# A decoder block's first stage: column sums on TensorE and VectorE against row sums from transposed weights on VectorE

## The chip, the cores and the metric

The kernel runs on one core of a Trainium2 chip. The metric is the device time of one execution in microseconds (us), given as the median of several runs; a profile of one execution supplies all durations of single instructions. The core's engines are TensorE (PE, matmuls; PEld is its weight load), VectorE (DVE), ScalarE (ACT), GpSimd (POOL) and SyncE (SP), which issues the DMA transfers. Each works through a queue of its own in the order of the program and waits on semaphores of the others.

## The reference

One decoder block on 1024 tokens of width 1024, batch 1, all in fp32. Only the first lines concern the change; attention and MLP follow.

```python
cond = jax.nn.silu(c)
mod = (cond @ w_ada[l] + b_ada[l]).astype(x.dtype)          # 1024 -> 6 * 1024
sh_a, sc_a, gt_a, sh_m, sc_m, gt_m = [m[:, None, :] for m in jnp.split(mod, N_MOD, axis=-1)]
h = rms_norm(x, g_attn_pre[l]) * (1 + sc_a) + sh_a
proj = h @ w_in[l]                                          # 1024 -> 2304
...
y = mixed @ w_out[l]                                        # after two attentions, with RoPE on q and k
x = x + gt_a * rms_norm(y, g_attn_post[l])
h = rms_norm(x, g_mlp_pre[l]) * (1 + sc_m) + sh_m
y = jnp.square(jax.nn.relu(h @ w_up[l])) @ w_down[l]
x = x + gt_m * rms_norm(y, g_mlp_post[l])
```

## The kernel before

A scheduler in Python writes the whole program. Each piece of work is an `op` with an engine (or a choice of two), an estimated duration, the ops it depends on and the buffers it takes and gives back; a planner with its own clock then lays down the order of every engine's queue. So a change in one piece can move instructions that it does not touch. Rings of buffers are counted by `Res` objects: `r_stg` and `r_wa` for loaded 512 KB pieces, `r_w` for split weights, `r_t`, `r_x`, `r_pj`, `r_o`, `r_s` for the eight PSUM banks (tags t, x, pj, o, s). Loads made with `in_turn` are issued strictly in the order of the code.

Products that need fp32 accuracy are made of three matmuls. Each operand is split into a high part (rounded by a cast on ScalarE) and a low part (the rest, by a subtraction); then high x high, high x low and low x high add up in one bank. Lines 773, 774 and 776 are these three.

The first stage, up to the first scores at about 93 us:

- **x**: eight blocks of 128 rows. Each is squared and summed on ScalarE (L571), `rs_t` is formed on VectorE (L409), its power -1/2 on GpSimd (L412), the block is scaled (L575 on ScalarE or L576 on VectorE), transposed by eight matmuls (L583, `pxt`), and copied into `xnT` (L587), the transposed x.
- **Angles** of RoPE: 27 dependent steps on 64 elements a partition, on GpSimd (L539 to L546), some last ones on VectorE (L552 to L555), then sine tables on ScalarE (L559 to L561).
- **Modulation**: the first 2048 columns of w_ada (shift and scale of attention) come in four groups of columns, each in four pieces of 512 KB. Some pieces go through TensorE against `cond` with one column moving (L609, table `BY_PE`); the others are multiplied by a column of cond and added up on VectorE (L624, L626 into `acc_a`), and the sum over partitions is a matmul against ones (L635). L640 to L642 make the scale `g_a` and the shift `s_a` of two chunks of 128 columns.
- **Modulated block**, for each chunk k of 128 columns: the high part of `xnT * g_a + s_a` on ScalarE (L652, `hw`), the full value on VectorE (L655), the low part on GpSimd or VectorE (L658).
- **Weights**: w_in is cut into six units of 384 columns (two heads of one kind with their keys and values, or four with one key head). A unit's eight chunks are loaded (L477 and on, `w_st`), split into `w_hl` by a cast on ScalarE (L494) and a subtraction (L499, for unit 0 on GpSimd).
- **Projection of unit 0**: seven of the eight row blocks (`FIRST`) accumulate side by side, each in a bank of its own (`acc_at`), for chunks 0 to 5 chunk by chunk; chunks 6 and 7 follow row block by row block (`AHEAD` = 6), so that the first block is done early. The eighth row block is a normal tile. Each finished block goes to ScalarE and VectorE, through rotation, transposes of q and k (`pq` L726, `pk` L738, in bank x) and on to the scores (`s_ps`, L999).

Units 1 to 5 and the two attentions are then interleaved, until about 450 us; the output projection and the MLP follow.

## Time and profile before

| what | us |
|---|---|
| median of 3 runs (1200.5 to 1203.06) | 1202.58 |
| span of the profiled execution, first to last instruction | 1198.4 |
| first cast of a modulated chunk (L652) starts | 30.7 |
| last one starts | 70.4 |
| first scores (L999) | 92.77 |
| mean granted TensorE clock over the span | 0.978 |

The page cuts the span into 40 slices of 30 us. Each digit is the busy share of a slice in tenths.

```profile
PE   6889999999998998999899999999999999999996
DVE  5867768666779897666888965479763797646998
POOL 5536455565655333111100000000000000000002
PEclk8689999999999999999999999999999999999999
DMA  9512332323331413555297127951268511585103
```

The change concerns the first three digits. In the second slice, 30 to 60 us, TensorE's granted clock is 0.6.

### The profile page before, as it was taken

Reading aid. Unit: us, or ns where it says so; the run is one execution under the profiler, and the core shown is the slowest. Engines: PE = TensorE matmul, PEld = TensorE weight load, DVE = VectorE, ACT = ScalarE, POOL = GpSimd, SP = SyncE. Lnnn points to the kernel's source line nnn. Section 1 sums busy time; section 2 is a strip of 40 time slices with the busy share of each in tenths; the row PEclk is TensorE's granted clock in tenths of the full one; section 3 lists DMA queues with packets and bytes.
Section 4 is the critical chain, followed back from the end, with each engine's and each line's share of the span. In section 5 each row is a group of like instructions: output and inputs, shape, how many; then the busy total and the mean of one; then the engine's idle time right before and its main releaser. Section 6 shows DMA issues by size and latency. Waiting matters only on the chain.

```text
span 1198.4 us, 17398 instructions
## 1 busy us (share of the span) xinstructions
PE 1148.6 (96%) x6060; PEld 1001.4 (84%) x6060; DVE 885.4 (74%) x1773; ACT 660.2 (55%) x1390; POOL 266.1 (22%) x322
## 2 busy tenths in 40 slices
PE   6889999999998998999899999999999999999996
PEld 5888999989998896888688888888888888888885
DVE  5867768666779897666888965479763797646998
ACT  6328666566566787567657533474324643246542
POOL 5536455565655333111100000000000000000002
PEclk8689999999999999999999999999999999999999
DMA  9512332323331413555297127951268511585103
GB/s 311 167 56 64 88 99 77 85 62 91 87 87 54 121 52 80 180 186 209 105 380 261 36 71 227 339 180 55 78 224 285 193 36 53 177 286 221 36 18 141
DMA packets 96488, 166.54 MB, mean 139 GB/s; under 512 B 11408, under 2 KB 48400, under 8 KB 96400
## 3 DMA queue, kind: packets, MB, share of 16 engines
q1 hardware_dynamic: 96400, 165.42, 41.3%
q8 instruction: 48, 0.79, 0.3%
q14 instruction: 40, 0.33, 0.1%
HBM read 137.08 MB, written 28.31 MB: 138 GB/s over the span
## 4 chain that ended last, share of the span: by engine, by line
PE 74%; DVE 13%; ACT 4%; issue 4%; POOL 3%; DMA 3%; SPq 0%; DVEq 0%; POOLq 0%; ACTq 0%
PE mlp_ps L1775 16%; PE mlp_ps L1776 16%; PE mlp_ps L1774 16%; PE pj L773 3%; PE pj L776 3%; PE pj L774 3%; PE s_ps L999 3%; DVE acc_a L626 2%; PE o_ps L1133 1%; DMA wa<-in_w_ada 1%; PE pt_ps L1102 1%; PE y_ps L1350 1%; PE y_ps L1352 1%; PE y_ps L1351 1%; PE pt_ps L1105 1%
## 5 line engine op out<-in xcount | busy, mean ns | idle before, releaser
L1774 PE MATMUL mlp_ps<-hw 128*128 128x512 f32 x896 | 350.3, 391 | 0.4 <-ACT hw L1536 0.4
L1775 PE MATMUL mlp_ps<-hw 128*128 128x512 f32 x896 | 349.2, 390 | 1.1 <-DVE hw L1542 1.1
L1776 PE MATMUL mlp_ps<-hw 128*128 128x512 f32 x896 | 349.1, 390 | 0.0
L1775 PEld LDWEIGHTS mlp_ps<-hw 128*128 128x128 f32 x896 | 168.5, 188 | 36.8 <-DVE hw L1542 1.4
L1774 PEld LDWEIGHTS mlp_ps<-hw 128*128 128x128 f32 x896 | 168.6, 188 | 36.2 <-ACT hw L1536 0.8
L1776 PEld LDWEIGHTS mlp_ps<-hw 128*128 128x128 f32 x896 | 168.5, 188 | 35.0
L1545 DVE TENSOR_TENSOR hw<-w,hw 128x1024 fp32r<-128x1024 f32 x96 | 114.8, 1223 | 94.0 <-ACT hw L1538 92.5
L1538 ACT CAST hw<-w 128x1024 fp32r<-128x1024 f32 x96 | 97.6, 1048 | 129.6 <-PE mlp_ps L1776 93.0
L1874 POOL TENSOR_TENSOR st<-st,nhalf 128x1 f32<-128x1 f32 x8 | 7.8, 978 | 602.8 <-DVE st L1872 602.8
L773 PE MATMUL pj<-w_hl,hw 128*128 128x384 f32 x328 | 121.9, 372 | 4.1 <-DVE sk L719 4.1
L776 PE MATMUL pj<-w_hl,hw 128*128 128x384 f32 x328 | 111.3, 339 | 0.0
L774 PE MATMUL pj<-w_hl,hw 128*128 128x384 f32 x328 | 111.1, 339 | 0.0
L1538 ACT CAST hw<-u 128x1024 fp32r<-128x1024 f32 x48 | 48.7, 1054 | 64.5 <-PE mlp_ps L1776 64.5
L1120 DVE TENSOR_TENSOR ph<-pt_ps,ph 128x512 fp32r<-128x512 f32 (+1 forms) x110 | 69.2, 645 | 16.7 <-ACT ph L1116 16.2
L1545 DVE TENSOR_TENSOR hw<-u,hw 128x1024 fp32r<-128x1024 f32 x48 | 57.2, 1224 | 18.2 <-ACT hw L1538 18.2
L1116 ACT CAST ph<-pt_ps 128x512 fp32r<-128x512 f32 (+1 forms) x110 | 59.6, 561 | 14.8 <-PE pt_ps L1105 10.6
L773 PEld LDWEIGHTS pj<-w_hl,hw 128*128 128x128 f32 x328 | 62.2, 190 | 5.4 <-issue 2.9
L1029 POOL TENSOR_SCALAR p_sb<-p_sb,den 128x128 f32<-128x128 f32 (+3 forms) x64 | 49.2, 773 | 70.6 <-DVE den L1027 47.4
L1832 DVE TENSOR_TENSOR yacc<-yacc,mlp_ps 128x512 f32<-128x512 f32 x96 | 62.4, 688 | 3.3 <-PE mlp_ps L1776 3.3
L774 PEld LDWEIGHTS pj<-w_hl,hw 128*128 128x128 f32 x328 | 62.4, 190 | 1.2 <-issue 0.2
L776 PEld LDWEIGHTS pj<-w_hl,hw 128*128 128x128 f32 x328 | 62.0, 189 | 0.0
L1024 ACT ACTIVATE p_sb<-p_sb,mn 128x128 f32<-128x128 f32 (+3 forms) x64 | 50.0, 782 | 21.2 <-DVE mn L1017 17.7
(208 smaller groups left out, 2238.6 us busy)
## 6 DMA issues: line engine op xcount, KB each, us to landing
hw<-s_dram SPq DMA_DIRECT2D x84, 512.0 KB, 4.3
wa_st<-in_w_ada SPq DMA_DIRECT2D x32, 512.0 KB, 4.2
w<-in_w_up SPq DMA_DIRECT2D x32, 512.0 KB, 5.0
w<-in_w_down SPq DMA_DIRECT2D x32, 512.0 KB, 7.7
s_dram<-hw SPq DMA_DIRECT2D x28, 512.0 KB, 4.1
x_sb<-in_x SPq DMA_DIRECT2D x16, 512.0 KB, 6.1
wa<-in_w_ada SPq DMA_DIRECT2D x32, 256.0 KB, 5.8
w_st<-in_w_in SPq DMA_DIRECT2D x32, 192.0 KB, 4.7
```

The lines of the kernel that those rows point to most:

```text
L773: T.matmul(ps, hw[:, tb, 0, t], w[:, 0], start=(k == 0), stop=False)
L774: T.matmul(ps, hw[:, tb, 0, t], w[:, 1], start=False, stop=False)
L776: T.matmul(ps, hw[:, tb, 1, t], w[:, 0], start=False, stop=(k == KC - 1))
L1024: A.activation(rec.p[qi], rec.p[qi], AF.Exp, bias=b["mn"][:, m:m + 1], scale=-1.0, accum_out=b["den"][:])
L1116: A.copy(b["ph"][:, 0, :w], b["pt"][:, :w])
L1120: V.tensor_tensor(b["ph"][:, 1, :w], b["pt"][:, :w], b["ph"][:, 0, :w].bitcast(F32), ALU.subtract)
L1538: A.copy(out[j][0], flat(src[j]))
L1545: V.tensor_tensor(out[j][1], flat(src[j]), out[j][0].bitcast(F32), ALU.subtract)
L1774: T.matmul(ps[m][:], sh, mh, start=starts and k == 0, stop=False, **kw)
L1775: T.matmul(ps[m][:], sh, ml_, start=False, stop=False, **kw)
L1776: T.matmul(ps[m][:], sl, mh, start=False, stop=k == 3, **kw)
L1832: e = op("DVE", t_dv(512), lambda: V.tensor_tensor(y(), y(), ps[m][:], ALU.add), [e, ml.e_y[tb, n]], gives=gives, prio=1)
```

## The change

The host lays out two weights anew: w_in as contiguous tiles, one for each unit and chunk, and the first 2048 columns of w_ada transposed (`ada_t`: for each chunk, the output column is the partition and the 1024 inputs lie along it, once for the scale and once for the shift). With that the modulation of one output column is a sum along a partition: VectorE multiplies 128 x 1024 weights by `cond_b`, cond spread over all partitions, and adds up in the same instruction, starting from the bias (L606 of the changed kernel, `tensor_tensor_reduce`, twice a chunk). `cond_b` comes from eight matmuls of a diagonal matrix with ones.

All eight row blocks accumulate side by side in all eight banks. Block 0 takes the bank of tag x, which the transposes of q and k use later. The full value of the modulated block moves from VectorE to ScalarE, its low part and the low parts of unit 0's weights from GpSimd to VectorE, the angle steps from GpSimd to VectorE; the sine tables come after the last chunk. Unit 1's weights are loaded right behind unit 0's. Lines of the later stages stand about 24 lower than in the kernel before.

```diff
+    w = h["w_in"][0].reshape(KC, P, 2304)
+    parts = [[w[:, :, o + 128 * u:o + 128 * u + 128] for o in (768, 1280, 1792)] for u in range(4)]
+    parts += [[w[:, :, 256 * v:256 * v + 256], w[:, :, 512 + 64 * v:576 + 64 * v], w[:, :, 640 + 64 * v:704 + 64 * v]]
+              for v in range(2)]
+    h["w_in"] = np.ascontiguousarray(np.stack([np.concatenate(q, axis=2) for q in parts]))
+    a = h["w_ada"][0, :, 0:2 * D].reshape(P, KC, 2, KC, P)
+    h["ada_t"] = np.ascontiguousarray(a.transpose(3, 4, 2, 1, 0)).reshape(KC, P, 2 * D)
+    return {n: h[n] for n in ARGS}
...
-    FIRST = 7
+    FIRST = 8
...
+    cond_b = p0.tile([P, D], F32, name="cond_b")
+    NWA = 8
+
+    r_wa = Res(NWA)
     n_load = [0]
 
     def pri():
...
-    def load_ada(g, j):
-
-        def emit():
-            wa_t[g, j] = stage("wa") if j == 3 else place0("wa")
-            for n in range(2):
-                nc.sync.dma_start(
-                    wa_t[g, j][:, 512 * n:512 * n + 512].rearrange("p (i n) -> p i n", i=2),
-                    ada_view[:, 2 * j + n, 0:2 * D].rearrange("p (i n) -> p i n", i=2)[:, :, g * GW:g * GW + GW])
-        wa_e[g, j] = in_turn(emit, 524288, r_stg if j == 3 else r_wa)
+    def load_ada(k):
+        for i in (1, 0):
+            def emit(i=i):
+                wa_t[k, i] = place0("wa")
+                nc.sync.dma_start(wa_t[k, i][:], ada_t[k, :, i * D:i * D + D])
+            wa_e[k, i] = in_turn(emit, 524288, r_wa)
...
+    IN_STG = (0, 1, 2)
...
+            nc.sync.dma_start(t[:], w_in[u, k])
...
-            w_e[u, k] = op("POOL", t_ptt(UW), lo(G), [e], gives=[(r_wst, 1)], prio=3)
+            w_e[u, k] = op("DVE", t_dv(UW), lo(V), [e], gives=[(r_wst, 1)], prio=1)
...
+    e_posi = load(lambda: nc.sync.dma_start(posi[:], positions), 4096, prio=pri())
     load_x(0)
-    e_posi = load(lambda: nc.sync.dma_start(posi[:], positions), 4096, prio=pri())
     for tb in range(1, TB):
         load_x(tb)
-    for g in range(4):
-        for j in range(4):
-            load_ada(g, j)
-        for k in range(2):
-            load_w(0, 2 * g + k)
+    for k in range(KC):
+        load_ada(k)
+        load_w(0, k)
...
+    cond_ps, diag = [], []
+
+    def f_diag():
+        diag.append(by_k(place0("diag")))
+        for j in range(KC):
+            V.tensor_scalar(diag[0][:, j], ident, cond[:, j:j + 1], None, ALU.mult)
+    e = op("DVE", 1.3, f_diag, [e_cond], takes=[(r_wa, 1)], prio=0)
+
+    def f_cps():
+        for i in range(2):
+            cond_ps.append(pt.tile([P, 512], F32, name="cond_ps", tag="t"))
+            for j in range(4):
+                T.matmul(cond_ps[i][:, j * P:(j + 1) * P], ones[:], diag[0][:, 4 * i + j], start=True, stop=True)
+    e = pe_op("mod", 2.0, f_cps, [e, e_init], takes=[(r_t, 2)], gives=[(r_wa, 1)])
+
+    def f_cb():
+        for i in range(2):
+            A.copy(cond_b[:, 512 * i:512 * i + 512], cond_ps[i][:])
+    e_cb = op("ACT", 2 * t_ps(512), f_cb, [e], gives=[(r_t, 2)], prio=0)
...
-        e = op("POOL", 0.34, f, [e, e_c], prio=8)
+        e = op("DVE", 0.12, f, [e, e_c], prio=8)
...
-            junk = p0.tile([P, D], BF16, name="junk", tag="junk", bufs=1)
-            A.activation(junk[:], x_t[tb][:], AF.Square, accum_out=ssq[:, tb:tb + 1])
+            A.activation(xnT[:, :, tb * P:(tb + 1) * P], x_t[tb][:].rearrange("p (j n) -> p j n", n=P), AF.Square,
+                         accum_out=ssq[:, tb:tb + 1])
...
-    BY_PE = ((0, 2), (0,), (0,), (0,))
...
-            def f(j=j, first=first):
-                for n in range(2):
-                    w, cj = wa_t[g, j][:, 512 * n:512 * n + 512], cond[:, 2 * j + n:2 * j + n + 1]
-                    if first and not n:
-                        b["acc"] = p0.tile([P, 512], F32, name="acc_a", tag="acc_a", bufs=2)
-                        V.tensor_scalar(b["acc"][:], w, cj, None, ALU.mult)
-                    else:
...
+    e_hh, e_hl, e_full = {}, {}, [None]
+
+    def mod_chunk(k):
+
+        def gemv(i, dst, first):
+            def f():
+                w = wa_t[k, i]
+                V.tensor_tensor_reduce(w[:], w[:], cond_b[:], 1.0, first, ALU.mult, ALU.add, dst)
+            return f
+        c1 = g_a[:, k:k + 1]
+        e1 = op("DVE", t_dv(D) + AP_DV, gemv(1, c1, bb[:, k, 1:2]), [wa_e[k, 1], e_cb, e_cols],
+                gives=[(r_wa, 1)], prio=2)
+        e1 = op("DVE", 0.07, lambda: V.tensor_tensor(c1, c1, cols[:, 8 + k:9 + k], ALU.mult), [e1], prio=1)
+        e2 = op("DVE", t_dv(D) + AP_DV, gemv(0, s_a[:, k:k + 1], bb[:, k, 0:1]), [wa_e[k, 0], e_cb, e_cols],
+                gives=[(r_wa, 1)], prio=2)
...
-            V.tensor_scalar(h, h, g_a[:, k:k + 1], s_a[:, k:k + 1], ALU.mult, ALU.add)
-
-        def lo(eng):
-            return lambda: eng.tensor_tensor(hw[:, :, 1, ks], hb, hw[:, :, 0, ks].bitcast(F32), ALU.subtract)
-        e_hh[k] = op("ACT", t_sb(S) + 2 * AP_COST, hi, [eg] + e_xn, prio=0)
-        e = op("DVE", t_d2(S) + 2 * AP_DV, full, [e_hh[k]], prio=0)
-        e_hl[k] = op(("DVE", "POOL"), (t_dv(S), t_ptt(S)), (lo(V), lo(G)), [e], prio=0)
+            A.activation(h, h, AF.Identity, bias=s_a[:, k:k + 1], scale=g_a[:, k:k + 1])
+
+        def lo():
+            V.tensor_tensor(hw[:, :, 1, ks], hb, hw[:, :, 0, ks].bitcast(F32), ALU.subtract)
+        e_hh[k] = op("ACT", t_sb(S) + 2 * AP_COST, hi, [e1, e2] + e_xn, prio=0)
+        e = e_full[0] = op("ACT", t_sb(S) + 2 * AP_COST, full, [e_hh[k]], prio=0)
+        e_hl[k] = op("DVE", t_dv(S), lo, [e], prio=0)
...
-    for g in range(4):
-        mod_group(g)
+    for k in range(KC):
+        mod_chunk(k)
+
+    def f_sin():
+        A.activation(sinw[:, :, 1], ang[:], AF.Sin)
+        A.activation(cosw[:], kq[:], AF.Sin)
+        A.activation(ang[:], kq[:], AF.Exp)
+    e = op("ACT", 3.0, f_sin, [e_ang, e_full[0]], prio=8)
+    e_rope = op("DVE", 0.15, lambda: V.tensor_scalar(sinw[:, :, 0], sinw[:, :, 1], -1.0, None, ALU.mult), [e],
+                prio=8)
...
-    acc_at = [(pj, "pj", r_pj)] * 2 + [(po, "o", r_o)] + [(psp, "s", r_s)] * 2 + [(pt, "t", r_t)] * 2
+    acc_at = [(px, "x", r_x)] + [(pj, "pj", r_pj)] * 2 + [(psp, "s", r_s)] * 2 + [(po, "o", r_o)] + [(pt, "t", r_t)] * 2
...
-                      after=tick if part else None)
+                      gives=[(r_w, 1)] if part and tb == TB - 1 else [], after=tick if part else None)
...
-                load_w(u + 1, k, prio=-10 + k / 10)
+                load_w(u + 1, k, prio=-10 + k / 10 if u else None)
                 split_w(u + 1, k)
+
+    next_unit_w(0)
...
-            if tb == TB - 4 or u == 0:
+            if tb == TB - 4:
```

VectorE's order in the middle of the first stage, before: `acc_a` is the running sum over pieces of w_ada, `xnT` the transposed x, `bb` the bias; the rows end one group of two chunks and begin the next.

```order
L640 TENSOR_TENSOR g_a<-pm,bb 128x2
L641 TENSOR_TENSOR g_a<-g_a,head 128x2
L642 TENSOR_TENSOR s_a<-pm,bb 128x2
L624 TENSOR_SCALAR acc_a<-wa,cond 128x512
L626 SCALAR_TENSOR_TENSOR acc_a<-wa,cond,acc_a 128x512
L655 TENSOR_SCALAR xnT<-xnT,g_a,s_a 128x1024
L626 SCALAR_TENSOR_TENSOR acc_a<-wa,cond,acc_a 128x512 x2
```

The same place after the change; each `ISA` row of 128x1024 is one sum, the one of 128x1 the reading of its result.

```order
L606 ISA wa,g_a<-wa,cond_b,bb 128x1024
L606 ISA g_a 128x1
L495 TENSOR_TENSOR w_hl<-w_st,w_hl 128x384
L611 TENSOR_TENSOR g_a<-g_a,head 128x1
L606 ISA wa,s_a<-wa,cond_b,bb 128x1024
L606 ISA s_a 128x1
L624 TENSOR_TENSOR hw<-xnT,hw 128x8x128
```

The pieces of 512 elements for two chunks became sums of 1024 for one; the low parts L624 and L495 came in from GpSimd, and the full value L655 went out to ScalarE.

TensorE's order between the last three blocks' transposes and the first projection matmuls, before (`pm` are results of the modulation, `pxt` the transposes, numbers tell buffers apart):

```order
L583 MATMUL pxt_357<-head_65,x_sb_186 128x128 x4
L583 MATMUL pxt_366<-head_65,x_sb_186 128x128 x4
L609 MATMUL pm_381<-cond_69,wa_301 128x1 x8
L583 MATMUL pxt_406<-head_65,x_sb_188 128x128 x4
L583 MATMUL pxt_414<-head_65,x_sb_188 128x128 x4
L635 MATMUL pm_425<-ones_67,acc_a_353 128x1 x4
L583 MATMUL pxt_433<-head_65,x_sb_194 128x128 x4
L583 MATMUL pxt_445<-head_65,x_sb_194 128x128 x4
L609 MATMUL pm_451<-cond_69,wa_363 128x1 x8
L773 MATMUL acc_483<-w_hl_431,hw_126 128x384
L774 MATMUL acc_483<-w_hl_431,hw_126 128x384
```

And after:

```order
L591 MATMUL pxt_363<-head_65,x_sb_199 128x128 x4
L591 MATMUL pxt_376<-head_65,x_sb_199 128x128 x4
L591 MATMUL pxt_383<-head_65,x_sb_201 128x128 x4
L591 MATMUL pxt_395<-head_65,x_sb_201 128x128 x4
L747 MATMUL acc_414<-w_hl_381,hw_126 128x384
L748 MATMUL acc_414<-w_hl_381,hw_126 128x384
L747 MATMUL acc_422<-w_hl_381,hw_126 128x384
L748 MATMUL acc_422<-w_hl_381,hw_126 128x384
```

The modulation's matmuls are gone from between the transposes, and the projection follows the last transpose; ahead of all transposes stand eight matmuls for `cond_ps`.

GpSimd's order where the angle steps end, before:

```order
L545 TENSOR_SCALAR km<-kq 128x64
L412 TENSOR_TENSOR rstd<-rs_t,nhalf 128x1
L546 TENSOR_TENSOR ang<-ang,km 128x64
L499 TENSOR_TENSOR w_hl<-w_st,w_hl 128x384 x2
L658 TENSOR_TENSOR hw<-xnT,hw 128x8x128 x2
```

And all of it after, up to the first work on the later columns of w_ada (L860):

```order
L420 ISA
L420 TENSOR_TENSOR rstd<-rs_t,nhalf 128x1 x8
L495 TENSOR_TENSOR w_hl<-w_st,w_hl 128x384 x7
L860 TENSOR_SCALAR ada_acc<-wa_st,cond 128x512
L864 TENSOR_SCALAR wa_st<-wa_st,cond 128x512
```

The powers follow one another without angle steps between them, and the low parts of the block have left; the seven L495 belong to unit 1.

More of the change, by code (lines that the diff above doesn't have):

```diff
@@ L304, in hybrid_block @@
 def hybrid_block(ctx: ExitStack, tc: tile.TileContext, x, positions, w_ada, b_ada, g_attn_post, w_in, w_out,
-                 g_mlp_post, w_up, w_down, consts, out):
+                 g_mlp_post, w_up, w_down, ada_t, consts, out):
     nc = tc.nc
@@ L309, in hybrid_block @@
     x, out = x[0], out[0]
-    w_ada, w_in, w_out, w_up, w_down = w_ada[0], w_in[0], w_out[0], w_up[0], w_down[0]
+    w_ada, w_out, w_up, w_down = w_ada[0], w_out[0], w_up[0], w_down[0]
     sc = Sched()
@@ L556, in hybrid_block @@
     e = op("DVE", 0.8, f_ang, [e], prio=8)
-    def f_sin():
-        A.activation(sinw[:, :, 1], ang[:], AF.Sin)
-        A.activation(cosw[:], kq[:], AF.Sin)
-        A.activation(ang[:], kq[:], AF.Exp)
-    e = op("ACT", 3.0, f_sin, [e], prio=8)
-    e_rope = op("DVE", 0.15, lambda: V.tensor_scalar(sinw[:, :, 0], sinw[:, :, 1], -1.0, None, ALU.mult), [e],
-                prio=8)
+    e_ang = e
     e_xn = []
@@ L812, in proj_tile @@
                 gives.append((r_wo, 1))
-            d = dense(0.49, emit, [w_e[u, k]] + ([e_hh[k], e_hl[k]] if u == 0 else []), takes=[(r_pj, 1)] if k == 0 else [], gives=gives, after=tick)
+            d = dense(0.49, emit, [w_e[u, k]], takes=[(r_pj, 1)] if k == 0 else [], gives=gives, after=tick)
         evac(u, tb, lambda: b[0], d, r_pj)
-    todo_dense = [(u, tb) for u in range(6) for tb in range(FIRST if u == 0 else 0, TB)]
+    todo_dense = [(u, tb) for u in range(1, 6) for tb in range(TB)]
     def next_unit_w(u):
```

71 lines of the change are left out of this document (8 added, 63 removed).

## The prediction

> **What bounds the kernel now.** I read the page's engine row first, then a table of busy time by stretches of the span, then the first stage by its timeline. An engine's field in the table is busy us (instructions); the last three fields are TensorE's granted clock, the share of the DMA engines, and GB/s.
>
> ```profile
> PE 1148.6 (96%) x6060; PEld 1001.4 (84%) x6060; DVE 885.4 (74%) x1773; ACT 660.2 (55%) x1390; POOL 266.1 (22%) x322
> 20.00:30.00 10.00, 9.07 (x48) 8.86 (x47) 6.96 (x21) 6.74 (x11) 3.96 (x9) 0.59 1.09 333
> 30.00:40.00 10.00, 9.57 (x37) 9.24 (x36) 7.83 (x9) 3.67 (x5) 4.89 (x3) 0.55 1.11 338
> 40.00:50.00 10.00, 7.77 (x33) 7.80 (x34) 7.82 (x10) 3.19 (x4) 6.70 (x4) 0.62 0.51 158
> 50.00:60.00 10.00, 9.51 (x55) 9.17 (x54) 8.43 (x13) 3.12 (x4) 6.16 (x4) 0.84 0.01 2
> 60.00:70.00 10.00, 6.80 (x34) 6.51 (x33) 7.87 (x9) 0.86 (x2) 7.06 (x4) 0.84 0.07 7
> 95.00:340.00 245.00, 239.25 (x1709) 230.44 (x1708) 177.55 (x610) 157.34 (x470) 137.11 (x153) 0.99 0.28 80
> 340.00:450.00 110.00, 103.54 (x702) 98.32 (x701) 99.28 (x338) 81.15 (x276) 47.10 (x65) 1.00 0.30 86
> ```
>
> TensorE is busy 96% of the span and 98% of the attention stage (239.25 of 245). So work saved on another engine counts only where TensorE waits or runs at a low clock, and that is the stretch from 20 to 70: the clock is 0.55 to 0.84, and TensorE issues 33 to 55 matmuls in 10 us, against 70 in 10 us later (1709 in 245). The loads do not set this pace: at 50 to 70 they are silent (2 and 7 GB/s). VectorE is the busiest engine beside TensorE there. What paces it shows in the rows of the modulated block's cast on ScalarE, L652, two chunks at a time, and in what stands beside it.
>
> ```profile
> 44.49 2.38 ACT L652 ACTIVATE hw<-xnT,s_a,g_a 128x1024 fp32r<-128x1024 f32 x2 [10.59 <-DVE s_a L642]
> 56.88 2.38 ACT L652 ACTIVATE hw<-xnT,s_a,g_a 128x1024 fp32r<-128x1024 f32 x2 [9.20 <-DVE s_a L642]
> L652 ACT ACTIVATE hw<-xnT,s_a,g_a x8: 1228/1238/1247, 30.7 to 70.4; 128x1024 fp32r<-128x1024 f32 x8
> 34.42 3.52 DVE L626 SCALAR_TENSOR_TENSOR acc_a<-wa,cond,acc_a 128x512 f32<-128x512 f32 x2
> 34.58 2.81 POOL L658 TENSOR_TENSOR hw<-xnT,hw 128x1024 fp32r<-128x1024 f32 x1 [3.75 <-DVE xnT L655]
> 57.22 0.75 DVE L626 SCALAR_TENSOR_TENSOR acc_a<-wa,cond,acc_a 128x512 f32<-128x512 f32 x1
> ```
>
> Two chunks take 12.4 us (44.49 to 56.88), and ScalarE waits about 9 of them for VectorE's s_a. VectorE is slow because GpSimd works beside it: two L626 take 3.52 us while GpSimd's L658 runs, and one alone takes 0.75. So 2.0 us are lost beside one GpSimd step of 2.81, 72% of it. The first stage is bound by VectorE in its quarrel with GpSimd; TensorE's low clock follows from being starved.
>
> For the sum I need a mark that both kernels have: the end of unit 0's 192 projection matmuls of 384 columns (8 blocks, 8 chunks, 3 each).
>
> ```profile
> 94.91 0.34 PE L776 MATMUL pj<-w_hl,hw 128*128 128x384 f32 x1
> 92.47 0.46 PE L738 MATMUL pk<-ident_r,sk 128*128 128x128 f32 x4
> 92.77 0.41 PE L999 MATMUL s_ps<-kt,qt 128*128 128x128 f32 x2
> ```
>
> The 192nd starts at 94.91 and ends at **95.25**. By then before has also done 24 small matmuls of the next step (8 pq, 12 pk, 4 s_ps); in the changed order 6 of them (2 pq, 4 pk) stand ahead of the mark. The other 18 are owed, at about 0.11 each (four in 0.46): 2.0 us.
>
> **The change part by part.** *x first, GpSimd clear.* In before, the last block of x waits.
>
> ```profile
> 17.19 1.06 ACT L571 ACTIVATE junk<-x_sb 128x1024 bf16<-128x1024 f32 x1
> 22.23 0.55 POOL L412 TENSOR_TENSOR rstd<-rs_t,nhalf 128x1 f32<-128x1 f32 x1
> 22.81 1.15 ACT L575 ACTIVATE x_sb<-x_sb,rstd 128x1024 f32<-128x1024 f32 x1 [4.00 <-POOL rstd L412]
> 21.67 3.40 PE L609 MATMUL pm<-cond,wa 128*128 128x1 f32 x16 [0.93 <-PE pxt L583]
> 28.24 1.95 PE L583 MATMUL pxt<-head,x_sb 128*128 128x128 f32 x8
> 30.22 0.59 ACT L587 COPY xnT<-pxt 128x512 f32<-128x512 f32 x1 [0.27 <-PE pxt L583]
> ```
>
> Its square is done at 18.25, its power only at 22.78: it stood behind angle steps in GpSimd's queue. TensorE's order holds 1-column matmuls ahead of transposes of x (3.40 us for 16), and the first L652 starts at 30.7. The changed order has neither. The same chain without them: 18.3 + power step 0.8 + scaling 1.15 + transposes 1.95 + copy 0.59 = 22.8; with two blocks' queues on each engine I take 25, so 5 to 6 us sooner. The squares now write 4 bytes an element instead of 2; I cost that at nothing, since they wait for the loads anyway. Building the broadcast of cond (8 VectorE multiplies, 8 matmuls, 2 copies) lies under the loads of x.
>
> *The sums.* Sixteen VectorE instructions, 128x1024, two fp32 operands in SBUF, multiply and add up into one column. Before has no such row. The nearest are the same instruction with one operand in PSUM (L1017, here the forms that start from a column as the new one does) and plain two-operand steps in SBUF without the adding up.
>
> ```profile
> L1017 DVE CUSTOM_DVE_ANT_0 p_sb<-s_ps,masks,mn 128x128 f32<-128x128 f32 x8 | 2.7, 342 | 0.4
> L1017 DVE CUSTOM_DVE_ANT_0 p_sb<-s_ps,masks,mn 128x512 f32<-128x512 f32 x8 | 6.0, 748 | 0.6 <-PE s_ps L999 0.2
> L1228 DVE SCALAR_TENSOR_TENSOR hw<-wo_st,head,hw x5: 1276/1281/1493, 400.5 to 446.5; 128x1024 fp32r<-128x1024 f32 x5
> L658 DVE TENSOR_TENSOR hw<-xnT,hw x1: 1226/1226/1226, 74.3 to 74.3; 128x1024 fp32r<-128x1024 f32 x1
> ```
>
> The slope is (748 - 342)/384 = 1.06 ns an element, so 1024 elements give 748 + 512 x 1.06 = 1.29 us; the steps in SBUF give 1.23 to 1.28. I take **1.25** as the distance from one sum to the next (the reading of the column lies beside the next instruction's start). The ends: 1.2 below; above, twice that, 2.5, if the adding up cannot keep pace with two operands in SBUF. Three rows at one element in about 1.06 to 1.2 ns say the lower end. The Trainium skill ("Vector Engine (DVE) Microarchitecture Reference", section 7, "Points that are easy to get wrong") states that `S2S2D2_STT` "with two non-bf16 SBUF sources halves throughput", because no read port is left for the accumulator. L1228 and L626 are of that family, without an accumulator, and run at full rate (1281 for 1024), so the trace bears it out only if the adding up is meant; by it each sum would take about twice as long, and the time would be that of the first rival.
>
> *VectorE's chain to the last low part.* The first sum can start where the first piece of w_ada is worked on in before, at 20.05, since the same 4 MB of x come ahead. From there the order gives VectorE 16 sums, 8 multiplies of g (about 0.15), 9 low parts of weights, 8 low parts of the block (these go from GpSimd to VectorE) and 13 angle steps (0.23 from one to the next).
>
> ```profile
> 20.05 0.48 DVE L624 TENSOR_SCALAR acc_a<-wa,cond 128x512 f32<-128x512 f32 x1
> 23.10 0.20 DVE L552 TENSOR_SCALAR ang<-ang 128x64 f32<-128x64 f32 x1 [1.52 <-POOL ang L546]
> L499 POOL TENSOR_TENSOR w_hl<-w_st,w_hl x32: 996/1020/1475, 28.7 to 388.0; 128x384 fp32r<-128x384 f32 x32
> L499 DVE TENSOR_TENSOR w_hl<-w_st,w_hl x16: 540/666/1494, 104.6 to 391.6; 128x384 fp32r<-128x384 f32 x16
> ```
>
> That is 16 x 1.25 + 8 x 0.15 + 9 x 0.5 + 8 x 1.2 + 13 x 0.23 = 20.0 + 1.2 + 4.5 + 9.6 + 3.0 = 38.3 (0.5 being L499's minimum with some overlap of starts). Add 0.7 for copies of x still in the queue, and 1.5 for GpSimd: its low parts of unit 1's weights (L499 on GpSimd) are 1.0 us each, four of the seven come before the last chunk's cast in the order, and at 72% loss these cost 0 to 2.9, of which I take half. The Trainium skill ("SBUF — State Buffer", "Who interferes with whom") calls the port pair shared by VectorE and GpSimd an exclusive lock; by that all of those four steps could be lost, some 4 us, where this trace shows 72% of a step. The last low part then ends at 20.05 + 38.3 + 0.7 + 1.5 = **60.5**.
>
> *The other engines keep up.* A chunk lasts 38.3/8 = 4.8 us on VectorE. ScalarE has two casts of 1.24 a chunk (the full block comes to it from VectorE) and one or two of a weight at 0.5, 3.5 us at most; a chunk's loads are 1.25 MB, at 333 GB/s 3.7 us. TensorE has 24 matmuls a chunk (first row: the weight's cast; then matmuls of both clocks, and two windows).
>
> ```profile
> L494 ACT CAST w_hl<-w_st 128x384 fp32r<-128x384 f32 x8 | 3.7, 505 | 0.0
> 50.29 0.52 PE L773 MATMUL acc<-w_hl,hw 128*128 128x384 f32 x1
> 50.61 0.52 PE L774 MATMUL acc<-w_hl,hw 128*128 128x384 f32 x1
> 88.20 0.33 PE L773 MATMUL acc<-w_hl,hw 128*128 128x384 f32 x1
> 88.38 0.33 PE L774 MATMUL acc<-w_hl,hw 128*128 128x384 f32 x1
> 247.10:250.50 3.40, 3.40 (x15) 3.21 (x14) 0.88 (x4) 0.86 (x4) 3.20 (x4) 0.50 0.03 12
> 250.50:253.90 3.40, 3.40 (x28) 3.29 (x27) 1.29 (x2) 2.07 (x7) 0.00 (x0) 1.00 0.03 5
> ```
>
> One follows another in 0.32 at the low clock and in 0.175 at the full: 7.7 or 4.2 us a chunk. The last two rows show one stretch at the low clock: 3.4 us at 0.50, in which TensorE is busy throughout, then 1.00; it costs half of 3.4, 1.7 us. At the low clock TensorE falls behind here too, is then busy without a gap, and should get the full clock after such a stretch; there it keeps pace. Between 25 and 60.5 it has 149 matmuls to do, 0.24 each, so the low clock may take up to 0.4 of the time.
>
> *Tail.* Chunks 6 and 7 go block by block, so after the last low part stand 1 + 7 x 6 = 43 matmuls: 7.5 us, and 1.7 for one stretch at the low clock. The 192nd ends at 60.5 + 7.5 + 1.7 = 69.7, plus 2.0 owed: **71.7 against 95.25, 23.5 us sooner.**
>
> ScalarE's sine tables move behind the last chunk and ahead of the first rotation. In before they take from 24.94 to 28.21.
>
> ```profile
> 24.94 1.28 ACT L559 ACT_TABLE_LOAD   x1
> 27.95 0.26 ACT L561 ACTIVATE ang<-kq 128x64 f32<-128x64 f32 x1
> ```
>
> The 43 matmuls (7.5 us) hide these 3.3 us; without that cover they would come on top.
>
> *What is given back.* From the mark on, the attention stage is planned anew, with the same matmuls. TensorE is idle for 5.75 + 6.46 = 12.2 us in the two windows from 95 to 450. That is the most the new plan could gain; for the most it could lose I take the same gaps once more. So the ends are -12 and +12. I take **+6**, a loss: all eight blocks come due for VectorE and ScalarE within the 43 matmuls, few of the transposes and no score has begun (their bank holds block 0 until then), and VectorE is 90% busy later on (99.28 of 110), so it cannot hand the whole shift on. From the output projection on TensorE's order is the same in both. Loads of w_in in whole rows and unit 1's loads early only take work off a stage that no load bounds: nothing.
>
> Sum: -23.5 + 6 = **-17.5**. The profiled span is 1198.4 and the median of the runs 1202.58, 4.2 above it; 1198.4 - 17.5 = 1180.9 in the span, **1185** in the median.
>
> **The rivals.**
> *A, half rate:* each sum costs 2.35 to 2.5. Sixteen times 1.1 is 17.6: the gain is gone, 1202. For it: no row shows an accumulating step with both operands in SBUF. Against it: L1017 pays nothing for accumulating. Chance 0.05.
> *B, the other side:* the same sums at about 3.5 us, if writing back the product and the accumulator both slow it down. Then VectorE's chain grows by 16 x 2.25 = 36, and 36 - 17.5 gives 1221. It decides from 2.35 us a sum on. No row is that slow but L626 beside GpSimd (1.76 for 512 elements, that is 3.5 for 1024). Chance 0.04.
> *C, the gain is given back:* TensorE stays at the low clock in most chunks (each stretch at the low clock costs about 1.7; six more are 10 us), or the attention's new plan loses the full 12 instead of 6. For it: the clock of 0.55 to 0.84 now. Against: attention is 98% busy. 1185 + 6 to 10: 1191 to 1196. Chance 0.13.
> *D, the change does not do what it says*, GpSimd still collides: the order leaves it only the powers and seven steps, so I fold this into C.
>
> **How the numbers follow.** My forecast has 0.78: a give-back of 0 to 10 and one stretch of the clock either way put it between 1177 and 1191. The range reaches up through C to 1197; it leaves out A, B and the far tails, about 0.15. About 0.2% (2.4 us) is what a measurement can tell from no change. Faster: the forecast and C, 0.91; same: A, 0.05; slower: B, 0.04.
>
> **What would show it.** Right: L606 rows near 1.25 to 1.3 us, without growth beside GpSimd; the first cast of a chunk (L618) at about 25, the last at about 57 to 59; the 192nd matmul near 70; VectorE close to 100% busy from 20 to 60. Wrong: sums of 2.4 or more (A, B), a granted clock below 0.7 throughout 30 to 60, or TensorE idle far above 12 us in the attention stage (C).

## The result, and the profile after

The changed kernel takes **1181.29 us** (median of 4 runs, 1177.44 to 1184.43) against 1201.54 in the same comparison: ratio 0.9835, 95% interval 0.9807 to 0.9862. In a second comparison it was 1180.41 against 1202.7, ratio 0.9816 (0.9797 to 0.9834). The forecast was 1185, with a range of 1177 to 1197.

The page's engine row and the table of stretches of the changed kernel, in the columns known from the prediction:

```profile
PE 1121.8 (95%) x5964; PEld 975.4 (83%) x5964; DVE 885.0 (75%) x1812; ACT 670.4 (57%) x1400; POOL 232.2 (20%) x279
20.00:30.00 10.00, 6.67 (x28) 5.79 (x27) 9.16 (x19) 9.06 (x12) 0.39 (x1) 0.74 0.97 331
30.00:40.00 10.00, 10.00 (x54) 10.00 (x54) 10.00 (x20) 7.09 (x8) 0.00 (x0) 0.92 1.03 404
40.00:50.00 10.00, 10.00 (x59) 10.00 (x59) 10.00 (x17) 7.81 (x11) 1.40 (x1) 1.00 0.32 100
50.00:60.00 10.00, 4.69 (x26) 4.02 (x24) 9.76 (x14) 6.31 (x10) 8.37 (x7) 0.95 0.60 193
60.00:70.00 10.00, 8.08 (x36) 8.07 (x37) 6.81 (x32) 4.92 (x20) 6.58 (x7) 0.71 0.12 46
75.00:320.00 245.00, 238.83 (x1739) 230.88 (x1738) 180.58 (x627) 160.26 (x478) 128.61 (x144) 1.00 0.27 78
320.00:430.00 110.00, 102.94 (x691) 96.63 (x689) 99.95 (x345) 81.97 (x279) 46.48 (x67) 1.00 0.26 77
```

From 30 to 50 TensorE now runs at 0.92 and 1.00 instead of 0.55 and 0.62, VectorE is busy 10.00 of 10 and GpSimd nearly silent. From 50 to 60 the picture turns: GpSimd is busy 8.37, and TensorE falls to 4.69.

The operations that answer to those of before, by line (duration minimum/median/maximum in ns, then first and last start in us), the last matmul of unit 0, and the first scores:

```profile
L606 DVE CUSTOM_DVE_ANT_0 wa<-wa,cond_b,bb x16: 1277/1280/2039, 18.7 to 49.6; 128x1024 f32<-128x1024 f32 x16
L618 ACT ACTIVATE hw<-xnT,s_a,g_a x8: 1230/1242/1247, 24.2 to 54.5; 128x1024 fp32r<-128x1024 f32 x8
71.63 0.34 PE L750 MATMUL acc<-w_hl,hw 128*128 128x384 f32 x1
77.06 0.41 PE L975 MATMUL s_ps<-kt,qt 128*128 128x128 f32 x2
```

A sum takes 1.28 us. The first chunk's cast starts at 24.2 (30.7 before), the last at 54.5 (70.4), and unit 0 ends at 71.97 (95.25). Marks of both profiles, in us:

| mark | before | changed | difference |
|---|---|---|---|
| 192nd matmul of unit 0 ends | 95.25 | 71.97 | -23.3 |
| last scores of the first attention (L999; L975 in the changed kernel) start | 340.7 | 316.1 | -24.6 |
| output projection starts | 463.6 | 440.6 | -23.0 |
| MLP starts | 568.1 | 545.9 | -22.2 |
| span | 1198.4 | 1175.3 | -23.1 |

What is won at the first mark arrives at the end, within 2 us. The profiled execution was the fastest of its four; by medians the gain is 20 to 22.

What VectorE did at the end of the stage, with GpSimd's row of the same time:

```profile
48.60 6.82 POOL L495 TENSOR_TENSOR w_hl<-w_st,w_hl 128x384 fp32r<-128x384 f32 x4 [28.22 <-ACT w_hl L490]
49.57 2.04 DVE L606 CUSTOM_DVE_ANT_0 wa<-wa,cond_b,bb 128x1024 f32<-128x1024 f32 x1
51.54 2.04 DVE L624 TENSOR_TENSOR hw<-xnT,hw 128x1024 fp32r<-128x1024 f32 x1
53.50 0.95 DVE L611 TENSOR_TENSOR g_a<-g_a,head 128x1 f32<-128x1 f32 x1
54.48 1.35 DVE L495 TENSOR_TENSOR w_hl<-w_st,w_hl 128x384 fp32r<-128x384 f32 x1
56.23 1.06 DVE L560 TENSOR_TENSOR ang<-ang,km 128x64 f32<-128x64 f32 x1
57.81 0.99 DVE L559 TENSOR_SCALAR km<-kq 128x64 f32<-128x64 f32 x1
58.84 0.95 DVE L560 TENSOR_TENSOR ang<-ang,km 128x64 f32<-128x64 f32 x1
60.65 1.22 DVE L624 TENSOR_TENSOR hw<-xnT,hw 128x1024 fp32r<-128x1024 f32 x1
```

The reader is to see two things. Steps that take 1.28, 1.22, 0.15, 0.55, 0.19 and 0.22 elsewhere are 0.73 to 0.84 us longer here; these are the seven rows up to 60, for GpSimd's seven steps, 5.5 us in all. And the last L624, for which TensorE waits, stands behind the angle steps (L559, L560) in VectorE's queue.

### The profile page after: what moved, and what is told of

It is laid out like the page before. It is cut to its first block, busy times and chain, and to the rows that moved or that the text cites. A ratio compares the mean times of both kernels' runs of the same rounds, so it can differ in the third digit from the quotient of the medians.

```text
span 1175.3 us, 17156 instructions
## 1 busy us (share of the span) xinstructions
PE 1121.8 (95%) x5964; PEld 975.4 (83%) x5964; DVE 885.0 (75%) x1812; ACT 670.4 (57%) x1400; POOL 232.2 (20%) x279
## 4 chain that ended last, share of the span: by engine, by line
PE 62%; DVE 10%; ACT 3%; issue 3%; POOL 2%; DMA 1%; SPq 0%; DVEq 0%; POOLq 0%; ACTq 0%
PE mlp_ps L1751 16%; PE mlp_ps L1752 16%; PE mlp_ps L1750 16%; PE pj L747 2%; PE pj L750 2%; PE pj L748 2%; PE s_ps L975 1%; DMA o_sb<-o_dram 1%; DVE hw L1521 1%; PE y_ps L1326 1%; PE y_ps L1328 1%; PE o_ps L1120 1%; PE y_ps L1327 1%; DVE x_sb L1852 1%; DVE ph L1096 1%
## 5 line engine op out<-in xcount | busy, mean ns | idle before, releaser
L1750 PEld LDWEIGHTS mlp_ps<-hw 128*128 128x128 f32 x896 | 168.2, 188 | 36.8 <-ACT hw L1512 1.6
L747 PE MATMUL pj<-w_hl,hw 128*128 128x384 f32 x320 | 118.3, 370 | 4.6 <-DVE sk L693 4.6
L750 PE MATMUL pj<-w_hl,hw 128*128 128x384 f32 x320 | 108.1, 338 | 0.0
L748 PE MATMUL pj<-w_hl,hw 128*128 128x384 f32 x320 | 107.9, 337 | 0.0
L747 PEld LDWEIGHTS pj<-w_hl,hw 128*128 128x128 f32 x320 | 60.4, 189 | 6.3 <-issue 2.9
L748 PEld LDWEIGHTS pj<-w_hl,hw 128*128 128x128 f32 x320 | 60.6, 189 | 1.2 <-issue 0.2
L750 PEld LDWEIGHTS pj<-w_hl,hw 128*128 128x128 f32 x320 | 60.1, 188 | 0.0
```

The lines of the kernel that those rows point to most:

```text
L747: T.matmul(ps, hw[:, tb, 0, t], w[:, 0], start=(k == 0), stop=False)
L748: T.matmul(ps, hw[:, tb, 0, t], w[:, 1], start=False, stop=False)
L750: T.matmul(ps, hw[:, tb, 1, t], w[:, 0], start=False, stop=(k == KC - 1))
L1750: T.matmul(ps[m][:], sh, mh, start=starts and k == 0, stop=False, **kw)
```

## The experiments

Differences are against the changed kernel (1181.29, 1180.41) unless another is named; ratios are to the kernel before, with 95% intervals. Some edits only move work; since the planner orders everything anew, a difference of 1 or 2 us is not read.

**Is VectorE's chain the limit? (sums_twice)**

```diff
                 w = wa_t[k, i]
+                V.tensor_tensor(hw[:, :, 1, k * P:(k + 1) * P], by_k(w), by_k(cond_b), ALU.mult)
                 V.tensor_tensor_reduce(w[:], w[:], cond_b[:], 1.0, first, ALU.mult, ALU.add, dst)
```

The durations that the planner assumes for these steps are doubled with it.

> Every sum is preceded by a plain product of the same two operands (128x1024), whose result is overwritten later; the output stays the same. One such step is 1.14 us from start to start in the changed kernel, so VectorE's chain grows by 16 x 1.14 = 18 us. Theory (VectorE's chain sets the first stage, and the attention hands the shift on whole): last low part at about 80 instead of 61.9, unit 0's 192nd matmul near 90 instead of 72, time +18 us, 1199. Rival 1 (attention gives back a quarter of a shift, as the prediction's +6 of 23.5 had it): +13 to +14. Rival 2 (loads, ScalarE or TensorE pace the stage): under +9.

1199.48 us, ratio 0.9975 (0.9964 to 0.9987): +18 to +19. The first product and the first sum in this kernel, and the row with which unit 0 ended, 22 us later than in the changed kernel; the profiled span was 22.8 longer:

```profile
20.12 1.21 DVE L606 TENSOR_TENSOR hw<-wa,cond_b 128x1024 fp32r<-128x1024 f32 x1
21.37 1.28 DVE L607 CUSTOM_DVE_ANT_0 wa<-wa,cond_b,bb 128x1024 f32<-128x1024 f32 x1
93.77 0.41 PE L751 MATMUL acc<-w_hl,hw 128*128 128x384 f32 x1
```

A product costs 1.25 us from its start to that of the sum (21.37 - 20.12), not the 1.14 expected, so 20 us for sixteen; the first step also came 1.4 us later. The last low part ended 21 us later (83.1 against 61.9), which is both together: VectorE's work stands on the path with its full length. The shift at this mark is handed on nearly whole. Against the profile of changed_again, a second run of the changed kernel (mark 73.2, span 1179.5), it is 21.0 at the mark and 18.6 in the span, so that 2 or 3 us given back can't be excluded; rival 1 would have had 5. The run also shows the price of the prediction's rival A: with 1.25 us more a sum, nearly all of the gain is gone.

**GpSimd back in the chunk stage (low_parts_gpsimd)**

```diff
-        e_hl[k] = op("DVE", t_dv(S), lo, [e], prio=0)
+        e_hl[k] = op(("DVE", "POOL"), (t_dv(S), t_ptt(S)), (lo(V), lo(G)), [e], prio=0)
...
-            w_e[u, k] = op("DVE", t_dv(UW), lo(V), [e], gives=[(r_wst, 1)], prio=1)
+            w_e[u, k] = op("POOL", t_ptt(UW), lo(G), [e], gives=[(r_wst, 1)], prio=3)
```

> The block's low parts and unit 0's weight low parts go back to GpSimd (the planner may choose VectorE for the block's). Theory (GpSimd beside VectorE costs VectorE about three quarters of the GpSimd step): some 28 us of GpSimd work stretch VectorE's chain by about 21 and take about 13 off it; last low part some 8 us later, near 70, time +6 to +10, about 1189; sums beside GpSimd take 2 us or more. Rival (what counts is VectorE's own work, GpSimd does not matter): 10 to 13 us faster.

1187.3 us, ratio 0.9884 (0.9861 to 0.9907): +6 to +7. The sums by line in this kernel (count, busy us, mean ns):

```profile
L606 DVE CUSTOM_DVE_ANT_0 wa<-wa,cond_b,bb 128x1024 f32<-128x1024 f32 x16 | 31.8, 2010 | 0.0
```

VectorE has eight low parts of the block and unit 0's eight weight parts fewer, and is later all the same: the sums take 2.01 on average instead of 1.28, and TensorE's 192nd matmul ends at 78.2 instead of 72. The time is at the lower edge of its theory (+6 to +10).

**The same in the kernel before (before_low_vector)**: the block's low parts and unit 0's weight low parts pinned to VectorE, nothing else.

```diff
-            w_e[u, k] = op("POOL", t_ptt(UW), lo(G), [e], gives=[(r_wst, 1)], prio=3)
+            w_e[u, k] = op("DVE", t_dv(UW), lo(V), [e], gives=[(r_wst, 1)], prio=1)
...
-        e_hl[k] = op(("DVE", "POOL"), (t_dv(S), t_ptt(S)), (lo(V), lo(G)), [e], prio=0)
+        e_hl[k] = op("DVE", t_dv(S), lo(V), [e], prio=0)
```

> The kernel before, with the block's low parts and unit 0's weight low parts pinned to VectorE. Theory (VectorE lost its time beside GpSimd, not to its own work): per two chunks VectorE has six pieces of about 0.66, two full values of 0.74, two low parts of 1.14, two weight low parts of 0.47 and 0.8 of small steps, 9.7 us, against the 12.4 measured; three periods are 8 us shorter, time 6 to 9 us lower, 1193 to 1196; no piece above 0.8. Rival (VectorE's load counts, and it grows by 12 us): 4 to 8 us slower.

1186.05 us, ratio 0.9858 (0.9839 to 0.9877): 17 us faster than the kernel before, twice what was expected. The pieces of the modulation in the kernel before, then in this one (two casts, L626 by line, and the 192nd matmul):

```profile
L626 DVE SCALAR_TENSOR_TENSOR acc_a<-wa,cond,acc_a x18: 739/1060/2827, 20.6 to 66.2; 128x512 f32<-128x512 f32 x18
```

```profile
41.81 2.38 ACT L652 ACTIVATE hw<-xnT,s_a,g_a 128x1024 fp32r<-128x1024 f32 x2 [7.35 <-DVE s_a L642]
53.18 2.37 ACT L652 ACTIVATE hw<-xnT,s_a,g_a 128x1024 fp32r<-128x1024 f32 x2 [4.92 <-DVE s_a L642]
L626 DVE SCALAR_TENSOR_TENSOR acc_a<-wa,cond,acc_a x18: 741/752/753, 21.5 to 58.8; 128x512 f32<-128x512 f32 x18
81.97 0.34 PE L776 MATMUL pj<-w_hl,hw 128*128 128x384 f32 x1
```

No piece is above 0.753; GpSimd does nothing from 23.7 to 79.5. The last pair of casts came at 61.5 instead of 69.2, as expected (three periods 8 us shorter). TensorE, whose granted clock was 0.80 instead of 0.64 from 20 to 62, then had less left to do: the 192nd matmul ended at 82.3 instead of 95.25. That was not in the expectation. By medians, two lines in the old modulation thus give 17 of the change's 20 to 22 us. The profiled execution took 1190.53, 4.5 above the median: of the 12.9 us won at its mark, 9.6 arrive in its span. The other 3.3 are lost between the last scores of the first attention and the output projection, 126.6 us instead of 122.9 at a granted clock of 0.95 instead of 0.99.

**The eighth block (first7)**: `FIRST = 7` and the banks of before, with the eighth block as a tile.

```diff
-    FIRST = 8
+    FIRST = 7
...
-    acc_at = [(px, "x", r_x)] + [(pj, "pj", r_pj)] * 2 + [(psp, "s", r_s)] * 2 + [(po, "o", r_o)] + [(pt, "t", r_t)] * 2
+    acc_at = [(pj, "pj", r_pj)] * 2 + [(po, "o", r_o)] + [(psp, "s", r_s)] * 2 + [(pt, "t", r_t)] * 2
```

> Seven blocks side by side as before, the eighth as a tile behind. Theory (VectorE's chain sets the stage): the last low part stays near 62; behind it stand 1 + 36 matmuls and the eighth block's 24, 61 instead of 43, 3.2 us more of TensorE, though the transposes of q and k can start earlier: time +1 to +4, about 1184. Rival (eight side by side brings most of the gain by keeping TensorE busy at the full clock): +10 or more.

1182.23 us, ratio 0.9839 (0.9812 to 0.9867): not to be told from the changed kernel. But the last low part did not stay near 62. GpSimd's steps of unit 1 before 69, and the last low part:

```profile
48.58 3.84 POOL L495 TENSOR_TENSOR w_hl<-w_st,w_hl 128x384 fp32r<-128x384 f32 x2 [28.21 <-ACT w_hl L490]
56.27 1.22 DVE L624 TENSOR_TENSOR hw<-xnT,hw 128x1024 fp32r<-128x1024 f32 x1
```

Only two of these steps, not seven, ran beside VectorE's chain, which ended 4.4 us sooner (57.5); TensorE's longer tail took that back, and the 192nd matmul ended at 72.4 instead of 72.0. So two effects cancel here. The rival's 10 us or more is not seen, but what the eighth block by itself is worth was not measured; from these marks I estimate about 5 us (4.4 + 0.4).

**Angle steps back on GpSimd (angles_gpsimd)**

```diff
...
-        e = op("DVE", 0.12, f, [e, e_c], prio=8)
+        e = op("POOL", 0.34, f, [e, e_c], prio=8)
```

The lines left out put the 27 instructions themselves on GpSimd.

> The changed kernel with the 27 angle steps back on GpSimd. Theory (in the kernel before the powers of x stood behind angle steps, which made the first chunk late): the first chunk's cast comes 3 to 5 us later, at 27 to 29; VectorE is rid of 13 steps in the chunk stage (3 us), so the last low part moves by -1 to +2 and the time by 0 to +3, about 1183. Rival (the powers do not matter, the loads set the start): first cast at 24 to 25, last low part 3 us sooner, time 1 to 3 us lower.

1180.74 us, ratio 0.9827 (0.9799 to 0.9854): the same time. The last power, the first cast, and two steps from the end of VectorE's chain in this kernel:

```profile
22.07 0.55 POOL L420 TENSOR_TENSOR rstd<-rs_t,nhalf 128x1 f32<-128x1 f32 x1
25.23 1.25 ACT L618 ACTIVATE hw<-xnT,s_a,g_a 128x1024 fp32r<-128x1024 f32 x1
54.42 2.00 DVE L606 CUSTOM_DVE_ANT_0 wa<-wa,cond_b,bb 128x1024 f32<-128x1024 f32 x1
60.15 1.23 DVE L624 TENSOR_TENSOR hw<-xnT,hw 128x1024 fp32r<-128x1024 f32 x1 [1.72 <-ACT xnT L621]
```

The power is as late as in the kernel before (22.23), and yet the first cast starts at 25.2, one us later than in the changed kernel, not three to five. So the theory's start fell: powers behind angle steps account for about 1 of the 6.5 us there. Its end held: the last low part came at 61.4 (61.9 in the changed kernel), although no angle step stood ahead of it on VectorE. GpSimd's steps lengthened the last three sums instead (2.00 to 2.04), and the last cast came at 57.3 instead of 54.5.

**Unit 1's low parts off GpSimd (w1_on_vector)**

```diff
+        elif u == 1:
+            w_e[u, k] = op("DVE", t_dv(UW), lo(V), [e], gives=[(r_wst, 1)], prio=3)
```

> All low parts of unit 1's weights go to VectorE, none to GpSimd. In the changed kernel seven of them on GpSimd stand beside VectorE steps that are 0.75 to 0.82 us longer than elsewhere: about 5.6 us. Theory (each GpSimd step stretches VectorE's chain): no VectorE step above its usual length from 48 to 61; five more steps of 0.47 ahead of the last low part, so it ends about 3 us sooner, near 59, and the time is 2 to 4 us lower, about 1178. Rival (the stretching lies in time that VectorE would wait anyway): last low part not sooner than 61, time the same or up to 2 us longer.

1179.49 us, ratio 0.9806 (0.9786 to 0.9825): within the intervals of the changed kernel. But unit 0 ended 7 us sooner. What happened behind it:

```profile
60.75 0.19 DVE L571 TENSOR_SCALAR kq<-kq 128x64 f32<-128x64 f32 x1
61.10 1.28 ACT L638 ACT_TABLE_LOAD   x1
64.55 0.34 PE L752 MATMUL acc<-w_hl,hw 128*128 128x384 f32 x1
68.45 0.34 PE L702 MATMUL pq<-ident_r,sp 128*128 128x128 f32 x2 [3.57 <-DVE sk L695]
76.69 0.41 PE L977 MATMUL s_ps<-kt,qt 128*128 128x128 f32 x2
```

The seven us are lost between two of these rows. TensorE has nothing to do from 64.9 to 68.45, since the rotated k is not there: VectorE's last angle step ends at 60.9, and ScalarE begins the sine tables only at 61.1. Then its granted clock is 0.62 until 72.9, which costs another 1.7. The first scores start at 76.69, where the changed kernel had them at 77.06. A second limit lay right behind the first.

**Tables and angle steps sooner (tables_mid, w1_vec_tables_mid)**: the angle steps get a higher priority on VectorE, and the sine tables follow chunk 4 instead of the last. The second kernel has the edit of w1_on_vector too.

```diff
-        e = op("DVE", 0.12, f, [e, e_c], prio=8)
+        e = op("DVE", 0.12, f, [e, e_c], prio=2)
...
-        e = e_full[0] = op("ACT", t_sb(S) + 2 * AP_COST, full, [e_hh[k]], prio=0)
+        e = op("ACT", t_sb(S) + 2 * AP_COST, full, [e_hh[k]], prio=0)
+        if k < 5:
+            e_full[0] = e
...
-    e = op("ACT", 3.0, f_sin, [e_ang, e_full[0]], prio=8)
+    e = op("ACT", 3.0, f_sin, [e_ang, e_full[0]], prio=2)
```

> As w1_on_vector (unit 1's low parts on VectorE), and the angle steps come earlier on VectorE and the sine tables after chunk 4 instead of behind the last chunk. In w1_on_vector unit 0's 192nd matmul ended at 64.5, 7 us sooner than in the changed kernel, yet the first scores came at 76.7 against 77.1, and TensorE waited 3.6 us for the rotated k. Theory (the rotation's tables took over as the limit there): the first scores come at about 70 to 72, and the 7 us are handed on: time 1173 to 1176. Rival (the blocks' way out of the banks through ScalarE and VectorE is the limit, tables or not): first scores not before 75, time 1178 to 1181, as w1_on_vector.

> The changed kernel with only the earlier angle steps and the sine tables after chunk 4; unit 1's low parts stay with the planner's choice, mostly GpSimd. Theory (in the changed kernel two limits lie one behind the other: VectorE stretched by GpSimd, then the rotation's tables; each alone gives little): last low part near 58 to 61, time 1177 to 1181, 0 to 4 us lower than the changed kernel. Rival (the tables alone were the limit): 1171 to 1174, as w1_vec_tables_mid.

w1_vec_tables_mid: 1170.49 us, ratio 0.9736 (0.9717 to 0.9754), a little better than its theory. tables_mid, without the move to VectorE: **1170.11 us**, ratio 0.9728 (0.9712 to 0.9744), as its rival had it, and my theory of two limits that give little each fell. The end of the stage in tables_mid:

```profile
51.38 2.04 DVE L624 TENSOR_TENSOR hw<-xnT,hw 128x1024 fp32r<-128x1024 f32 x1
53.34 1.00 DVE L642 TENSOR_SCALAR sinw<-sinw 128x64 f32<-128x64 f32 x1
54.38 1.95 DVE L624 TENSOR_TENSOR hw<-xnT,hw 128x1024 fp32r<-128x1024 f32 x1
70.48 0.44 PE L977 MATMUL s_ps<-kt,qt 128*128 128x128 f32 x2 [0.42 <-DVE sk L695]
```

GpSimd still stretches the last low parts (2.04 and 1.95 for 1.22). But no angle steps stand ahead of the last one, which ends at 56.3 instead of 61.9, and the tables are ready: the first scores come 6.6 us sooner, and the profiled span is 6.7 shorter. By medians the gain is 10.3 to 11.2, since the changed kernel's profile lies 3.9 below its median; against the profile of changed_again the two differences are 7.8 and 10.9. So some 3 us of the gain may lie behind the stage. The edit takes away both limits at once; moving the tables alone was not tried. Nearest to moving the steps alone is angles_gpsimd, which gained nothing.

**Variants.** w1_vec_angles_early is w1_on_vector with the angle steps first in VectorE's priority and the tables ahead of the first chunk, w1_vec_mid_gpang is w1_vec_tables_mid with the angle steps on GpSimd.

```diff
-        e = op("DVE", 0.12, f, [e, e_c], prio=8)
+        e = op("DVE", 0.12, f, [e, e_c], prio=0)
...
-    e = op("ACT", 3.0, f_sin, [e_ang, e_full[0]], prio=8)
+    e = op("ACT", 3.0, f_sin, [e_ang], prio=8)
```

> As w1_vec_tables_mid, but with the sine tables ahead of the first chunk's cast on ScalarE (3.3 us there). Theory (VectorE's chain sets the end of the stage, ScalarE has slack): first cast of a chunk 3 us later, near 27 to 28, last low part unchanged within 1 us, the same time as w1_vec_tables_mid. Rival (a late start of TensorE costs, since it then lags at the low clock): 2 to 4 us more than w1_vec_tables_mid.

> As w1_vec_tables_mid, with the angle steps on GpSimd, where they are done before unit 0's chunks. Theory (VectorE's chain still sets the stage): 13 steps of 0.23 leave the chain, the first chunk's cast is 1 us later, so the last low part comes about 2 us sooner and the time is 1 to 3 us lower, 1168 to 1170. Rival (VectorE's chain is no longer the limit, the blocks' way out of the banks is): the same 1170 to 1172.

w1_vec_angles_early: 1178.1 us, ratio 0.9793 (0.977 to 0.9815), 8 us above w1_vec_tables_mid; neither theory said so. The last scores of the first attention start at 311.0 in it and at 311.2 in w1_vec_tables_mid, so the stage is not the cause; the output projection starts at 441.5 against 434.6. The stretch between these two marks, here and then in w1_vec_tables_mid, in the columns known from the prediction:

```profile
311.00:441.50 130.50, 120.27 (x759) 112.69 (x758) 112.60 (x371) 92.80 (x308) 54.00 (x75) 0.92 0.27 83
311.20:434.60 123.40, 114.31 (x758) 106.93 (x757) 110.00 (x370) 92.53 (x307) 54.01 (x75) 0.97 0.30 88
```

The same matmuls keep TensorE busy 6.0 of the 7.1 us longer, at a granted clock of 0.92 instead of 0.97; the rest is idle time. Why the clock is lower in this order stays open.

w1_vec_mid_gpang: 1174.59 us, ratio 0.9768 (0.9752 to 0.9783), slower where 1 to 3 us less were expected: VectorE's first sum starts at 22.9 instead of 18.7, since the order puts it behind the scaling of x's last block, which waits for its power on GpSimd.

**The changed kernel again, and one more order (changed_again, w1_after_tables_mid)**: the second is tables_mid with unit 1's low parts planned behind the block's last low part.

```diff
-            w_e[u, k] = op(("DVE", "POOL"), (t_dv(UW), t_ptt(UW)), (lo(V), lo(G)), [e], gives=[(r_wst, 1)], prio=3)
+            w_e[u, k] = op(("DVE", "POOL"), (t_dv(UW), t_ptt(UW)), (lo(V), lo(G)),
+                           [e, e_hl[KC - 1]] if u == 1 else [e], gives=[(r_wst, 1)], prio=3)
```

> The changed kernel itself, so that its time and that of the next one come from one chip. Theory (its four runs, 1177 to 1184, scatter by a few stretches at the low clock): median 1179 to 1182, a profile between 1175 and 1181, the 192nd matmul of unit 0 near 72 again.

> As tables_mid, and unit 1's low parts wait for the last low part of the block. In tables_mid three VectorE steps beside GpSimd (two low parts of 1.95 to 2.04 instead of 1.22, and one of 1.00 instead of 0.2) were some 2.4 us longer. Theory (VectorE's chain still ends the stage): last low part ends near 54 instead of 56.3, time 1 to 3 us lower, 1167 to 1169. Rival (the blocks' way out of the banks and unit 1's late weights take over): 1170 or more, with TensorE waiting for w_hl of unit 1 or for the rotated k.

changed_again: 1180.41 us (1179.63 to 1181.61), the profile at 1179.5, unit 0's end at 73.2: as expected. w1_after_tables_mid: **1169.02 us**, ratio 0.9721 (0.9703 to 0.974), not to be told from tables_mid. The time fits its theory, but for no reason of that theory: GpSimd began unit 1's steps at 50.75 all the same (50.90 in tables_mid), as the planner's dependency puts no wait into its queue, and the last low parts again took 2.03 and 1.95. The dependency moved the plan, not the work, so that whether GpSimd's silence to the end would pay stays open.

## Why the prediction was right, and where its terms were off

**The bound.** That VectorE bounds the first stage, in its quarrel with GpSimd, held: before_low_vector shows it in the kernel before, low_parts_gpsimd and sums_twice in the changed one. That taking GpSimd's steps away there gives 17 of the change's 20 to 22 us was no part of the forecast.

**Start.** The first cast was put at 25 and came at 24.2. The reason given first, powers behind angle steps, is worth about 1 us (angles_gpsimd). What is left is the other one, the 1-column matmuls among the transposes, and the wait for the first group's scale; these were not tried apart.

**The sums.** 1.25 us from one to the next were assumed; the rows give 1.21 (36.84 - 35.63 and the like), 19.3 for sixteen. Rivals A and B are out. The mark of being right, no growth beside GpSimd, failed in one sum of sixteen (2.04). The rule of the Trainium skill ("Vector Engine (DVE) Microarchitecture Reference", section 7) that two non-bf16 sources in SBUF halve the pace beside the accumulator does not describe this instruction: it runs at 1.28 for 1024 elements with both.

**VectorE's chain.** Forecast end of the last low part: 60.5, measured 61.9. The sum is right by errors that cancel. The chain began at 18.7 instead of 20.05, its work was shorter (36.8 instead of 39.0, copies included, with 0.8 of waiting), and the term for GpSimd was **mis-sized: 1.5 forecast, with 2.9 as its upper end, 5.5 measured.** I counted four of the seven steps and took half of them as harmless. All seven met a step of VectorE, and each cost 0.73 to 0.84 for a GpSimd step that takes 1.0 undisturbed, whatever the VectorE step was. The Trainium skill ("SBUF — State Buffer", "Who interferes with whom") says that one of the two engines is blocked for the other's whole instruction, and that the order of issue decides which: the trace agrees in kind, shows 73 to 84% of a step lost, and GpSimd's steps grew too, four of them taking 6.82.

**Order of the tail.** I counted the angle steps by number and not by place. Twelve of the thirteen stood behind the last sum and ahead of the last low part, the one step that TensorE waits for, and in the very stretch in which GpSimd lengthens such steps (three of the twelve). So the last cast came at 54.5, not at 57 to 59 as forecast, and the last low part late all the same. "The 43 matmuls hide these 3.3 us" was said of the sine tables; in the changed kernel as it stands they nearly do, but w1_on_vector shows that the cover is used up: with a last low part 5 us sooner, the angles and the tables became the wait.

**Tail.** 10.1 us from the last low part to the 192nd matmul, forecast 9.2.

**Give-back.** This is the term that was off most. +6 was taken, between -12 and +12, because VectorE is 90% busy later on. Forecast mark and debt were -23.5; measured -23.3 + 2.0 = -21.3; the spans differ by 23.1, the medians by 20.3 and 22.3. In the profile of changed_again it is -22.1 + 2.0 = -20.1 at the mark and -18.9 in the span. So about nothing is given back, within 2 us, though VectorE is as busy later on as before (99.95 of 110). sums_twice shows nearly the same in the other direction. The forecast missed by 4 us: these 6, less the 2 by which the forecast mark was too early. That the term is nothing is what this order gave, not a rule: in the profile of before_low_vector 3.3 of 12.9 us were given back, and w1_vec_angles_early lost 7 us behind the stage, both at a lower granted clock. The bounds of 12 either way were wide enough; the +6 rested on a busy share (90%) and on no wait in a row.

## What to carry to other kernels

Before making an engine's work cheaper, look at who works beside it: keeping GpSimd's two-operand steps away from a busy VectorE, two lines in the old kernel, was worth, by medians, 17 us where a new algorithm brought 20 to 22. When one queue feeds the critical step, ask of each small step not only how long it is but whether it stands ahead of that step; here the place of some angle steps and a table load, moved together, was worth 10 us. And a shift on the path into a stage that is 98% busy came out at the end nearly whole in the change and in sums_twice, while other orders lost 3 to 7 us behind it: put such a give-back at nothing, with several us either way, unless a row shows a mechanism.
